# One unit of four and the mix of each row block transposed in float32 on TensorE instead of by DMA

## The chip, the cores and the metric

One core of a Trainium2 chip runs the whole program. The metric is the device time of one execution in microseconds. DMA stands for the core's sixteen DMA engines, SP for the engine that issues most of their transfers.

## The reference

One decoder layer is computed for a prompt of 1024 positions and for 8 single decode positions. The change lies in the prompt's attention and in what follows it:

```python
s_w = jnp.einsum('bqkgd,bskd->bqkgs', qi, wk[:, :, 0]) - sl5 * dist_w.astype(f32)[None, :, None, None, :]
o_w = jnp.einsum('bqkgs,bskd->bqkgd', masked_softmax(s_w, mask_w[None, :, None, None, :]), wk[:, :, 1])
...
o = gf[..., 0:1] * o_c + gf[..., 1:2] * o_s + gf[..., 2:3] * o_w
...
mix = jnp.concatenate([ya * jax.nn.silu(za), yb * jax.nn.silu(zb), yc * jax.nn.silu(zc)], axis=-1)
out = jnp.einsum('bte,ed->btd', mix, w_out)
return x + rms_norm(out, g_post).astype(x.dtype)
```

There are 8 heads of 64 and three branches: compressed (`o_c`), selected (`o_s`, here every block up to the position) and a window of 512 (`o_w`). All inputs and outputs are float32.

## The kernel before

Every float32 matmul is made of float16 ones: an operand is split into a high half (the float16 rounding) and a low half (the rest), and three products of halves are added. So each probability matrix and each mixed row exists twice in float16, high and low.

Attention starts at about 251 us. The 1024 positions are 8 row blocks of 128, taken in the order 7, 6, 2, 1, 0, 5, 4, 3 (`ROWS`, L1286). A row block is cut into **units** `u = (i, s0, nh)` of `nh` heads from head `s0`: one head each in rows 7 to 3, two in rows 2 and 1, four in row 0, 50 units in all (L1620). A unit of row i has `nh * nt` blocks of 128 x 128 probabilities, where `nt` is i + 1 plus min(i + 1, 5): 13, 12, 11, 10 and 8 for rows 7 to 3, 6 x 2, 4 x 2 and 2 x 4 for rows 2, 1, 0. The loop at L1660 runs a pipeline of four steps:

- `qk` (L1295): TensorE forms scores in PSUM tiles `s` of the pool `sp`, which has two slots of 128 x 1024. VectorE subtracts distances and takes the row bound (L1344), which frees the tile; ScalarE takes exponentials (L1346) into `P` and then copies all of `P`, scaled, to the float16 tile `H` (L1348).
- `high` (L1351): SP issues a DMA transpose of `H` into the first half of the tile `T` (L1355).
- `low` (L1358), one step later: VectorE forms `L`, the low half (L1362), and SP issues its DMA transpose into the second half of `T` (L1363).
- `pv` (L1382), three steps after `qk`: for each block three TensorE matmuls `O<-vn,T`, two with the high half and one with the low, into a tile of the pool `op`.

After four heads, `combine` (L1407) scales the sums (L1415); after eight, `finish` (L1418) adds the branches (L1422, L1423), multiplies by the gate `z` (L1425), and splits the product into halves (ScalarE L1429, VectorE L1431) that a DMA transpose (L1432) turns into `qa[:, i]`, the left operand of the output projection.

`outproj` (L1516) does 48 matmuls `op` of 128 x 512 for a row, 24 with pooling and gating rows (`mxg`, `mxp`) and 24 with `qa`. Projections of weights (`ps`), the pooling and gating branches and `outproj` are filler, which the loop hands out between units. The output weights are loaded by POOL's queue and split by ScalarE and VectorE (L1469).

The orders of TensorE, VectorE and ScalarE are set by a list scheduler in the framework, which goes by an estimate of times; SP and POOL keep the order of the program text. On every engine instructions run in order, so one that waits holds up those behind it. `fp` and `op` are two PSUM pools of two one-bank tiles each.

Of the kernel before, what the change touches and what calls it, by code (L numbers as in the profile page):

```python
# [10 lines left out]
F32 = mybir.dt.float32  # L11
F16 = mybir.dt.float16
I32 = mybir.dt.int32
AF = mybir.ActivationFunctionType
ALU = mybir.AluOpType
# [12 lines left out]
CE = {}  # L28
# [22 lines left out]
def tile_hymba(ctx: ExitStack, tc: tile.TileContext, A: dict):  # L51
    nc = tc.nc
    V, S, G, Y = nc.vector, nc.scalar, nc.gpsimd, nc.sync
    PS = bass.MemoryType.PSUM

    fp = ctx.enter_context(tc.tile_pool(name="fp", bufs=2, space=PS))
    sp = ctx.enter_context(tc.tile_pool(name="sp", bufs=2, space=PS))
# [8 lines left out]
    def mm(out, l, r, st, en):  # L66
        nc.tensor.matmul(out, lhsT=l, rhs=r, start=st, stop=en)  # L67
# [90 lines left out]
    qa = C.tile([128, 8, 8, 128], F16, name="qa")  # L158
# [38 lines left out]
    mp = D.tile([128, 2, 16], F32, name="mp")  # L197
# [208 lines left out]
    for c in range(3):  # L406
        a, b = c * CH, c * CH + CH
# [859 lines left out]
    AT = tc.alloc_tile_pool(name="AT", bufs=1, side="right", reuse_waits="tile")  # L1267
# [13 lines left out]
    def load_qx(i, hf):  # L1281
        t = qx[i, hf] = AT.tile([128, 2, 128], F16, tag="qx", name=f"qx{i}{hf}", bufs=2)
        for k in range(2):
            Y.dma_start(t[64 - k * 64:128 - k * 64], qa[k * 64:k * 64 + 64, i, hf * 4 + k:hf * 4 + 4:2])
# [4 lines left out]
    def spans(i):  # L1289
        n = min(i + 1, 5)  # L1290
        return (0, i + 1, 0), (1, n, i + 1)

    sums = {}

    def qk(u):  # L1295
        i, s0, nh = u
        nt = i + 1 + min(i + 1, 5)
        P = AT.tile([128, nh, nt * 128], F32, tag="P", name=f"P{i}_{s0}", bufs=2)
        if s0 == 0:
            sums[i] = AT.tile([128, 8, 4], F32, tag="sm", name=f"sm{i}", bufs=2)  # L1300
        sm = sums[i]
        if s0 == 0:
            load_qx(i, 1)
        elif s0 == 4 and i != ROWS[-1]:
            load_qx(ROWS[ROWS.index(i) + 1], 0)
        for h in range(nh):
            s = s0 + h
            k = s % 2
            r = slice(k * 64, k * 64 + 64)
            rx = slice(64 - k * 64, 128 - k * 64)  # L1310
            qy = qx[i, s0 // 4][rx, s % 4 // 2]
            lone = i == 7 and s < PARAM["lone"]
            slope = 2.0 ** -(SLOTS[s][0] * 4 + SLOTS[s][1] + 1)
            ps = None
            banks = []
            cuts = []
            for br, n, o in spans(i):
                T = n * 128
                if ps is None or n > 4 or i > 3:
                    ps = sp.tile([128, 1024], F32, tag="s", name=f"s{i}_{s}_{br}")  # L1320
                    z = 0
                else:
                    z = 512
                lo = (i + 1 - n) * 128
                if i > 3:
                    w = T // 2 if br else max(T // 2, 384)
                    z = 512 - w
                    parts = ((z, lo, w), (512, lo + w, T - w))
                else:
                    parts = ((z, lo, T),)  # L1330
                for a, c0, w in parts:
                    mm(ps[:, a:a + w], qa[:, i, s], ka[br][:, k, c0:c0 + w], True, False)
                    cuts.append((ps, br, a, c0, w))
                banks.append((ps, z))
            for pz, br, a, c0, w in cuts:
                if a == 512 and not lone:
                    mm(pz[:, a:a + w], qy, klx[br][rx, c0 - (384, 0)[br]:c0 - (384, 0)[br] + w], False, True)
                else:
                    mm(pz[:, a:a + w], qa[r, i, s], kl[br][r, c0:c0 + w], False, True)
            for (br, n, o), (ps, z) in zip(spans(i), banks):  # L1340
                T = n * 128
                end = 1024 if br == 0 else 1664
                p = P[:, h, o * 128:o * 128 + T]
                V.tensor_tensor_reduce(p, ps[:, z:z + T], ctt[:, end - T:end], -slope, 3e38, ALU.add, ALU.min,  # L1344
                                       sm[:, s, br:br + 1])
                S.activation(p, p, AF.Exp, bias=sm[:, s, br:br + 1], scale=-1.0, accum_out=sm[:, s, 2 + br:3 + br])  # L1346
        H = AT.tile([128, nh, nt * 128], F16, tag="H", name=f"H{i}_{s0}", bufs=2)
        S.activation(H, P, AF.Copy, scale=1024.0)  # L1348
        return P, H

    def high(u, P, H):  # L1351
        i, s0, nh = u
        nt = i + 1 + min(i + 1, 5)
        pt = AT.tile([128, 2 * nh * nt, 128], F16, tag="T", name=f"T{i}_{s0}", bufs=3)
        Y.dma_start_transpose(out=pt[:, 0:nh * nt], in_=H.rearrange("p h c -> p (h c)"))  # L1355
        return P, H, pt

    def low(u, P, H, pt):  # L1358
        i, s0, nh = u
        nt = i + 1 + min(i + 1, 5)  # L1360
        L = AT.tile([128, nh, nt * 128], F16, tag="L", name=f"L{i}_{s0}", bufs=2)
        V.scalar_tensor_tensor(L, P, 1024.0, H, ALU.mult, ALU.subtract)  # L1362
        Y.dma_start_transpose(out=pt[:, nh * nt:2 * nh * nt], in_=L.rearrange("p h c -> p (h c)"))  # L1363
        return pt
# [42 lines left out]
    def combine(i, h):  # L1407
        ob = obank.pop((i, h)).rearrange("p (s r d) -> p s r d", r=2, d=64)
        sc = AT.tile([128, 4, 2], F32, tag="asc", name=f"as{i}_{h}", bufs=2)
        V.scalar_tensor_tensor(sc, sums[i][:, h * 4:h * 4 + 4, 2:4], 1e-30, invg[:, i, h * 4:h * 4 + 4, 1:3],  # L1410
                               ALU.max, ALU.mult)
        V.reciprocal(sc, sc)
        if h == 0:
            mts[i] = AT.tile([128, 8, 2, 64], F32, tag="mt", name=f"mt{i}", bufs=1)
        V.tensor_tensor(mts[i][:, h * 4:h * 4 + 4], ob, sc.unsqueeze(3).to_broadcast([128, 4, 2, 64]), ALU.mult)  # L1415
        return finish(i) if h else None

    def finish(i):  # L1418
        t2 = mts.pop(i)
        t = t2[:, :, 0]  # L1420
        h3 = lambda x: x.rearrange("p (s d) -> p s d", d=64)
        V.tensor_tensor(t, t, t2[:, :, 1], ALU.add)  # L1422
        V.tensor_tensor(t, t, h3(ocs.pop(i)), ALU.add)  # L1423
        z = yza_t["z"][:, i]
        V.tensor_tensor(t, t, h3(z), ALU.mult)  # L1425
        t4 = t.rearrange("p (h s) d -> p h s d", h=2)
        hl = z.bitcast(F16)
        h5 = hl.rearrange("p (h a s d) -> p h a s d", h=2, a=2, d=64)
        S.activation(h5[:, :, 0], t4, AF.Copy)  # L1429
        yield  # L1430
        V.tensor_tensor(h5[:, :, 1], t4, h5[:, :, 0], ALU.subtract)  # L1431
        Y.dma_start_transpose(out=qa[:, i], in_=hl)  # L1432
        hold[f"ma{i}"] = qa[:, i]

    wo = {}
# [185 lines left out]
    for i in ROWS:  # L1621
        nh = (4, 2, 2, 1, 1, 1, 1, 1)[i]
# [37 lines left out]
    for st in range(n + 3):  # L1660
        t0 = now[0]
        flush()
        u = units[st - 1] if 1 <= st <= n else None
        if st < n:
            pend[units[st]] = qk(units[st])
        if u is not None:
            pend[u] = low(u, *pend[u])
        if st < n:
            pend[units[st]] = high(units[st], *pend[units[st]])
        bg_step()  # L1670
        if st >= n:
            bg_step()
            take(5.2)
        else:
            i, s0, nh = units[st]
            size = nh * (i + 1 + min(i + 1, 5))
            now[0] += 0.19 * size
            owed = take(owed + (PARAM["s2"] * size if "O" in outp else PARAM["s1"]) - 0.19 * size)
            now[0] = max(now[0], t0 + 0.33 * size + 0.8)
        if st >= 3:  # L1680
            v = units[st - 3]
            pv(v, pend.pop(v))
            e = v[1] + v[2]
            if e % 4 == 0:
                run_post(lambda: combine(v[0], v[1] // 4))
            if e == 8:
                fill.append(outproj(v[0]))
# [171 lines left out]
```

## Time and profile before

| | before |
|---|---|
| median of 3 runs | 587.06 us (586.46 to 589.16) |
| profiled execution, its time | 585.29 us |
| its span, first to last instruction | 583.5 us |
| TensorE matmuls busy | 519.7 us (89%) |
| VectorE, ScalarE, POOL busy | 441.8, 323.8, 197.0 us |
| mean granted TensorE clock | 0.953 |
| DMA transposes of `H` and `L` | 50 and 50, median 3.9 and 4.2 us to landing |

Times in rows of the trace count from the span's start. A busy TensorE is not TensorE at its peak: matmuls are pipelined, and a record is longer than the spacing of two. "DMA share" is the mean busy share of the sixteen DMA engines.

### The profile page before, as it was taken

How to read it: one execution, taken by the hardware profiler on the slowest of the kernel's cores; microseconds unless marked ns; L12 is line 12 of the kernel's file. 1: busy time of each engine (PE TensorE's matmuls, PEld its weight loads, DVE VectorE, ACT ScalarE, POOL GpSimd, SP SyncE). 2: the span in 40 equal slices, each digit the busy share in tenths (PEclk: the TensorE clock that was granted, in tenths of full speed). 3: DMA queues.
4: the chain of work that ended last, by engine and by line, in shares of the span. 5: the costliest groups of instructions: out<-in, count | busy, mean ns of one | idle time of the engine just before them, and what ended most of it. 6: DMA issues, size and time to landing. Idle time of an engine off the chain costs nothing. (4 is left out here: it accounts for less than half of the span.)

```text
span 583.5 us, 14199 instructions
## 1 busy us (share of the span) xinstructions
PE 519.7 (89%) x5716; PEld 342.7 (59%) x5716; DVE 441.8 (76%) x747; ACT 323.8 (55%) x574; POOL 197.0 (34%) x157
## 2 busy tenths in 40 slices
PE   5889988899999999899999979674599999998974
PEld 3566655589768999666666545442355455454531
DVE  5986489996686667478986987896799788768741
ACT  6444145564553434439656756496487765756600
POOL 1893179403267000045929775132011010000000
PEclk9989999899999999999999998967589999999997
DMA  8613984855675112847898597999969999998952
GB/s 300 260 37 99 253 222 135 244 165 143 206 260 159 39 40 34 239 92 145 171 184 166 97 184 114 125 229 224 124 100 166 182 213 206 177 215 153 199 154 80
DMA packets 199428, 95.31 MB, mean 163 GB/s; under 512 B 168890, under 2 KB 187738, under 8 KB 199362
## 3 DMA queue, kind: packets, MB, share of 16 engines
q1 hardware_dynamic: 195474, 80.85, 65.2%
q0 software_dynamic: 3744, 13.29, 7.3%
q8 instruction: 44, 0.72, 0.5%
q10 hardware_dynamic: 144, 0.26, 0.1%
q14 instruction: 22, 0.18, 0.1%
HBM read 45.43 MB, written 11.86 MB: 98 GB/s over the span
## 5 line engine op out<-in xcount | busy, mean ns | idle before, releaser
L67 PE MATMUL ps<-xh,ws 128*128 128x344 f16 x768 | 175.7, 313 | 5.8 <-DVE t L492 4.3
L67 PEld LDWEIGHTS <-ws 128*128 128x128 f16 x1376 | 129.3, 100 | 87.3 <-issue 17.4
L1346 ACT ACTIVATE P<-P,sm 128x640 f32<-128x640 f32 (+7 forms) x128 | 92.8, 725 | 77.6 <-DVE sm L1344 77.2
L67 PE MATMUL ps<-xl,ws 128*128 128x344 f16 x384 | 120.0, 313 | 0.0
L1362 DVE SCALAR_TENSOR_TENSOR L<-P,H 128x1024 f16<-128x1024 f32 (+4 forms) x50 | 85.0, 1700 | 25.7 <-ACT H L1348 15.3
L1344 DVE CUSTOM_DVE_ANT_0 P<-s,ctt 128x640 f32<-128x640 f32 (+7 forms) x128 | 84.8, 699 | 13.2 <-PE s L67 12.7
L67 PE MATMUL O<-vn,T 128*128 128x64 f16 x1584 | 64.0, 198 | 26.3 <-DMA T<-L 17.1
L67 PEld LDWEIGHTS <-T 128*128 128x128 f16 x1584 | 57.6, 101 | 40.4 <-DMA T<-L 18.9
L67 PEld LDWEIGHTS <-qa 128*128 128x128 f16 (+1 forms) x612 | 44.7, 98 | 61.5 <-issue 33.5
L1348 ACT ACTIVATE H<-P 128x1024 f16<-128x1024 f32 (+4 forms) x50 | 66.3, 1325 | 1.1
L67 PEld LDWEIGHTS <-xh 128*128 128x128 f16 x768 | 60.3, 98 | 0.7
L67 PE MATMUL op<-wo,qa 128*128 128x512 f16 x192 | 46.4, 389 | 3.3 <-DMA qa<-yza 3.3
L67 PE MATMUL s<-ka,qa 128*128 128x384 f16 (+4 forms) x192 | 45.1, 324 | 3.9 <-DVE sm L1344 3.7
L67 PE MATMUL zps<-ws,xh 128*128 128x128 f16 x512 | 45.0, 219 | 0.0
L1534 POOL TENSOR_SCALAR sq<-sq 128x1 f32<-128x1 f32 x8 | 3.9, 492 | 119.4 <-ACT o L1565 119.4
L67 PE MATMUL zps<-ws,xl 128*128 128x128 f16 x256 | 43.6, 219 | 0.0
L67 PEld LDWEIGHTS <-xl 128*128 128x128 f16 x384 | 37.5, 98 | 1.1 <-issue 0.5
L255 ACT ACTIVATE ws<-raw 128x1024 f16<-128x1024 f32 x21 | 22.2, 1056 | 17.6 <-PE ps L67 12.2
L67 PE MATMUL s<-kl,qa 64*128 64x384 f16 (+5 forms) x100 | 30.2, 329 | 0.0
L67 PE MATMUL s<-klx,qx 64*128 64x384 f16 (+4 forms) x92 | 26.9, 323 | 0.0
L1073 POOL TENSOR_TENSOR t<-t,yzc 128x1032 f32<-128x1032 f32 x2 | 4.8, 2382 | 60.4 <-DVE t L492 60.4
L67 PE MATMUL op<-wo,mxg 128*128 128x512 f16 x96 | 24.8, 395 | 0.1
(333 smaller groups left out, 917.5 us busy)
## 6 DMA issues: line engine op xcount, KB each, us to landing
raw<-in_wt_dram SPq DMA_DIRECT2D x21, 512.0 KB, 4.5
wor<-in_wo_dram POOLq DMA_DIRECT2D x8, 512.0 KB, 7.3
xr<-in_xn_dram SPq DMA_DIRECT2D x8, 512.0 KB, 4.8
o_y_dram<-o SPq DMA_DIRECT2D x7, 512.0 KB, 3.9
cr<-in_ccmp_dram SPq DMA_DIRECT2D x24, 128.0 KB, 3.3
o_kww_dram<-in_cwin_dram POOLq DMA_DIRECT2D x8, 259.0 KB, 4.5
o_kww_dram<-in_cwin_dram POOLq DMA_DIRECT2D x8, 252.0 KB, 4.8
xq<-in_xT_dram SPq DMA_DIRECT2D x3, 516.0 KB, 7.6
```

Of the source, the lines that this page charges most:

```text
L67: nc.tensor.matmul(out, lhsT=l, rhs=r, start=st, stop=en)
L255: S.activation(ws[:, 0, :, a:b], r, AF.Copy, scale=64.0)
L1073: G.tensor_tensor(t, t, hold.pop(f"zc{f2}"), ALU.mult)
L1344: V.tensor_tensor_reduce(p, ps[:, z:z + T], ctt[:, end - T:end], -slope, 3e38, ALU.add, ALU.min, sm[:, s, br:br + 1])
L1346: S.activation(p, p, AF.Exp, bias=sm[:, s, br:br + 1], scale=-1.0, accum_out=sm[:, s, 2 + br:3 + br])
L1348: S.activation(H, P, AF.Copy, scale=1024.0)
L1362: V.scalar_tensor_tensor(L, P, 1024.0, H, ALU.mult, ALU.subtract)
L1534: G.tensor_scalar(sq[:, 2:3], sq[:, 1:2], 1.0 / 1024, sq[:, 0:1], ALU.mult, ALU.add)
```

## The change

For one unit of four (the last head of each group of four in rows 7 to 3, the last unit in rows 2, 1 and 0: 13 units), `H`, `L` and both DMA transposes go. TensorE transposes `P` itself, in float32, block by block against an identity matrix, into tiles `tp` of the pool `sp`, up to eight blocks in one. ScalarE copies from there to the high half of `T`, and VectorE forms the low half. In `finish` of every row the gated product stays in float32 in `z`; TensorE transposes it in four blocks into a tile of `fp` (named `mp`), and ScalarE and VectorE split it out of PSUM into `qa`. The identity is loaded by SP before the first unit.

```diff
+    ident = AT.tile([128, 128], F32, name="ident")
+    Y.dma_start(ident, A["ce"][:, CE["ident"][0]:CE["ident"][0] + 128])
+
+    def by_pe(u):
+        i, s0, nh = u
+        return (s0 + nh) % 4 == 0 if i > 2 else s0 + nh == 8
...
+        if by_pe(u):
+            return P, None
         H = AT.tile([128, nh, nt * 128], F16, tag="H", name=f"H{i}_{s0}", bufs=2)
         S.activation(H, P, AF.Copy, scale=1024.0)
...
+        if by_pe(u):
+            return P, None, pt
         Y.dma_start_transpose(out=pt[:, 0:nh * nt], in_=H.rearrange("p h c -> p (h c)"))
...
+        if by_pe(u):
+            Pf = P.rearrange("p h c -> p (h c)")
+            for g in range(0, nh * nt, 8):
+                m = min(8, nh * nt - g)
+                tp = sp.tile([128, 1024], F32, tag="s", name=f"tp{i}_{s0}_{g}")
+                for j in range(m):
+                    nc.tensor.transpose(tp[:, j * 128:j * 128 + 128], Pf[:, (g + j) * 128:(g + j) * 128 + 128], ident)
+                t3 = tp.rearrange("p (j q) -> p j q", q=128)[:, 0:m]
+                hi = pt[:, g:g + m]
+                S.activation(hi, t3, AF.Copy, scale=1024.0)
+                V.scalar_tensor_tensor(pt[:, nh * nt + g:nh * nt + g + m], t3, 1024.0, hi, ALU.mult, ALU.subtract)
+            return pt
...
-        V.tensor_tensor(t, t, h3(z), ALU.mult)
-        t4 = t.rearrange("p (h s) d -> p h s d", h=2)
-        hl = z.bitcast(F16)
-        h5 = hl.rearrange("p (h a s d) -> p h a s d", h=2, a=2, d=64)
-        S.activation(h5[:, :, 0], t4, AF.Copy)
+        V.tensor_tensor(h3(z), t, h3(z), ALU.mult)
         yield
-        V.tensor_tensor(h5[:, :, 1], t4, h5[:, :, 0], ALU.subtract)
-        Y.dma_start_transpose(out=qa[:, i], in_=hl)
+        tp = fp.tile([128, 512], F32, tag="f", name=f"mp{i}")
+        for j in range(4):
+            nc.tensor.transpose(tp[:, j * 128:j * 128 + 128], z[:, j * 128:j * 128 + 128], ident)
+        t4 = tp.rearrange("p (a b q) -> p a b q", a=2, b=2)
+        m = qa[:, i].rearrange("p (a h b) q -> p a h b q", a=2, h=2)
+        S.activation(m[:, :, 0], t4, AF.Copy)
+        yield
+        V.tensor_tensor(m[:, :, 1], t4, m[:, :, 0], ALU.subtract)
```

The new text also moves instructions. On SP, from the last unit of row 2 to the third of row 1 (`T2_6` is the tile of row 2, head 6), there stood before:

```order
L1355 DMA_TRANSPOSE T2_6_5759<-H2_6_5754 128x12x128
L1284 DMA qx11_5849<-qa_87 64x2x128 x2
L1363 DMA_TRANSPOSE T2_6_5759<-L2_6_5872 128x12x128
L1355 DMA_TRANSPOSE T1_0_5875<-H1_0_5870 128x8x128
L1432 DMA_TRANSPOSE qa_87<-yza_2544 128x8x128
L1363 DMA_TRANSPOSE T1_0_5875<-L1_0_5959 128x8x128
L1355 DMA_TRANSPOSE T1_2_5962<-H1_2_5957 128x8x128
L1284 DMA qx00_6019<-qa_87 64x2x128 x2
L1363 DMA_TRANSPOSE T1_2_5962<-L1_2_6042 128x8x128
```

and in the same place stands now:

```order
L1284 DMA qx11_5901<-qa_87 64x2x128 x2
L1365 DMA_TRANSPOSE T1_0_5942<-H1_0_5922 128x8x128
L1385 DMA_TRANSPOSE T1_0_5942<-L1_0_6030 128x8x128
L1365 DMA_TRANSPOSE T1_2_6033<-H1_2_6028 128x8x128
L1284 DMA qx00_6091<-qa_87 64x2x128 x2
L1385 DMA_TRANSPOSE T1_2_6033<-L1_2_6114 128x8x128
```

Both transposes of row 2's last unit are gone, and so is the mix's, which stood between the two halves of row 1's first unit.

On VectorE, at the end of the program (what a row waits for stands in brackets), there stood before:

```order
L1362 SCALAR_TENSOR_TENSOR L3_7_8204<-P3_7_8144,H3_7_8154 128x1024 [waits DMAHW1_49,Activation_49]
L1566 TENSOR_TENSOR o324_8234<-op40_8166,gpb_6229 128x512 [waits Activation_49]
L1568 TENSOR_SCALAR sq4_8165<-sq4_8165 128x1
L1566 TENSOR_TENSOR o324_8234<-op41_8221,gpb_6229 128x512 [waits Activation_49]
L1415 TENSOR_TENSOR mt3_8140<-O3_1_8179,as3_1_8328 128x512 [waits DVE_49,PE_49]
L1539 SCALAR_TENSOR_TENSOR o324_8234<-o324_8234,sq4_8165,xr4_8163 128x1024 [waits DMAHW5_49,DVE_49,Pool_49]
L1422 TENSOR_TENSOR mt3_8140<-mt3_8140 128x8x64 [waits DVE_49]
L1423 TENSOR_TENSOR mt3_8140<-mt3_8140,ocs3_7942 128x8x64 [waits DVE_49]
L1425 TENSOR_TENSOR mt3_8140<-mt3_8140,yza_2544 128x8x64 [waits DVE_49]
L1431 TENSOR_TENSOR yza_2544<-mt3_8140,yza_2544 128x2x256 [waits Activation_49]
```

and now:

```order
L1590 TENSOR_TENSOR o324_8388<-op40_8312,gpb_6305 128x512 [waits DMAHW0_49,Activation_49]
L1592 TENSOR_SCALAR sq4_8311<-sq4_8311 128x1
L1381 SCALAR_TENSOR_TENSOR T3_7_8306<-tp3_7_0_8350,T3_7_8306 128x1024 [waits DMAHW7_49,DMAHW2_49,Activation_49]
L1590 TENSOR_TENSOR o324_8388<-op41_8375,gpb_6305 128x512 [waits Activation_49]
L1437 TENSOR_TENSOR mt3_8289<-O3_1_8325,as3_1_8482 128x512 [waits DVE_49,PE_49]
L1563 SCALAR_TENSOR_TENSOR o324_8388<-o324_8388,sq4_8311,xr4_8309 128x1024 [waits DMAHW6_49,DVE_49,Pool_49]
L1444 TENSOR_TENSOR mt3_8289<-mt3_8289 128x8x64 [waits DVE_49]
L1445 TENSOR_TENSOR mt3_8289<-mt3_8289,ocs3_8078 128x8x64 [waits DVE_49]
L1447 TENSOR_TENSOR yza_2544<-mt3_8289,yza_2544 128x512 [waits DVE_49]
L1456 TENSOR_TENSOR qa_87<-mp3_8489,qa_87 128x2x256 [waits Activation_49]
```

The low half of the last unit comes out of the PSUM tile `tp`, after one more step of row 4's output; the multiplication writes `yza` itself, and the last subtraction reads the PSUM tile `mp`. On TensorE the last unit's O matmuls are now followed by 12 projections of row 3, the four transposes into `mp`, 12 more projections, and the 24 that read `qa`. Row 7's mix is transposed within row 6, row 6's, 2's and 1's by the first units of row 5.

## Rows read from the trace of the kernel before

**Rows 1.** The page, busy tenths in 40 slices of the span.

```profile
PE   5889988899999999899999979674599999998974
PEclk9989999899999999999999998967589999999997
DMA  8613984855675112847898597999969999998952
```

**Rows 2.** Windows: length; PE, PEld, DVE, ACT, POOL busy; PEclk; DMA share; GB/s.

```profile
251.00:345.00 94.00, 90.64 (x1043) 59.22 (x1042) 80.70 (x116) 60.50 (x88) 66.20 (x31) 1.00 0.77 146
345.00:374.00 29.00, 25.36 (x301) 16.07 (x299) 22.99 (x53) 20.09 (x43) 9.77 (x10) 0.94 0.90 140
374.00:437.00 63.00, 39.66 (x435) 23.23 (x433) 50.08 (x130) 43.95 (x106) 13.04 (x13) 0.70 0.93 164
437.00:555.00 118.00, 114.42 (x1186) 59.97 (x1185) 93.96 (x175) 77.89 (x148) 8.37 (x13) 1.00 1.01 187
555.00:583.50 28.50, 16.65 (x121) 7.72 (x117) 8.79 (x15) 2.69 (x7) 1.61 (x4) 0.88 0.44 120
```

**Rows 3.** Timeline of TensorE at the decode step's four transposes; that window's row.

```profile
168.90 0.65 PE L817 MATMUL s<-cet,stl 128*128 128x128 f32 x4
...
169.39 0.31 PE L67 MATMUL ps<-xh,ws 128*128 128x344 f16 x1
...
168.00:170.50 2.50, 2.50 (x37) 2.01 (x35) 2.30 (x10) 0.55 (x3) 2.34 (x1) 1.00 1.01 390
```

**Rows 4.** Groups by line and shape: copies and splits, from SBUF and from PSUM.

```profile
L1348 ACT ACTIVATE H<-P 128x1664 f16<-128x1664 f32 x8 | 12.7, 1583 | 0.1
L1348 ACT ACTIVATE H<-P 128x1024 f16<-128x1024 f32 x14 | 14.8, 1054 | 0.3
L1362 DVE SCALAR_TENSOR_TENSOR L<-P,H 128x1024 f16<-128x1024 f32 x14 | 16.9, 1210 | 8.1 <-DMA T<-L 6.1 <-ACT H L1348 2.0
L576 ACT ACTIVATE thd<-cpsd 128x1024 f32<-128x1024 f32 x8 | 8.1, 1017 | 10.1 <-DVE ms L579 10.1
L577 DVE SCALAR_TENSOR_TENSOR thd<-thd,cpsd 128x1024 f32<-128x1024 f32 x8 | 9.7, 1215 | 0.0
```

**Rows 5.** Groups by line in 251 to 345: TensorE's first score matmuls.

```profile
L67 PE MATMUL s<-ka,qa 128*128 128x320 f16 (+2 forms) x59 | 13.7, 331 | 3.4 <-DVE sm L1344 3.3
```

**Rows 6.** Groups by line in 374 to 437; ScalarE's wait, from the list of waits.

```profile
L67 PE MATMUL O<-vn,T 128*128 128x64 f16 x228 | 13.2, 224 | 18.6 <-DMA T<-L 10.7 <-DMA T<-H 7.8
L67 PE MATMUL pp<-mxp,wpl 128*128 128x344 f16 x15 | 4.6, 436 | 4.4 <-ACT ocs L1380 4.4
...
ACT dsh L1162 <- DMA o_ps_dram<-dsh: 4.7, 1, 4.7
```

**Rows 7.** Timeline of SP's queue, 397 to 404: start, time in issue.

```profile
397.66 6.46 SPq L1432 DMA_TRANSPOSE qa<-yza  x1
```

**Rows 8.** The chain that ended last, in order of time: start, us, what.

```profile
552.71 0.04 ACT H L1348
...
565.72 0.64 ACT yza L1429
...
566.38 0.70 DVE yza L1431
...
567.10 3.04 DMA qa<-yza
570.18 6.96 PE op L67 x24
```

**Rows 9.** Timeline of TensorE at the end; in brackets the idle time before.

```profile
555.20 2.75 PE L67 MATMUL op<-wo,qa 128*128 128x512 f16 x12
557.79 0.92 PE L67 MATMUL O<-vn,T 128*128 128x64 f16 x26
560.89 0.81 PE L67 MATMUL O<-vn,T 128*128 128x64 f16 x22 [2.18 <-DMA T<-L]
...
570.18 6.94 PE L67 MATMUL op<-wo,qa 128*128 128x512 f16 x24 [3.29 <-DMA qa<-yza]
```

## The prediction

> **What bounds the kernel now.** I began with the forty slices [rows 1]: TensorE is at nine tenths in most of the second half, with a hole from slice 24 to 29 where its granted clock falls as well, while the DMA row stays near nine. Then I cut the attention, which is all that the change touches, into stages by the windows view [rows 2]; the reader is to see four different limits. In 251 to 345 (rows 7 and 6 with the last projections) TensorE is busy 90.6 of 94 us at full clock. In 374 to 437 (the end of row 2, rows 1 and 0, loading of the output weights) it is busy 39.7 of 63 us at a mean clock of 0.70; VectorE has 50 us, ScalarE 44, and the DMA share is 0.93. In 437 to 555 (rows 5, 4, 3 with the output projections) it is busy 114.4 of 118 us at full clock, and the DMA share is 1.01. After 555 comes a tail. The groups by line inside the hole say what TensorE waits for there: 18.6 us before the O matmuls, all of it for DMA transposes, and 4.4 us before a pooling matmul [rows 6]. The chain of waits and TensorE's timeline give the tail [rows 8, 9].
>
> **The change, part by part.** 13 of 50 units lose their two DMA transposes: two in each of rows 7, 6, 5, 4, 3 and one in each of rows 2, 1, 0. Their blocks number 2 x (13+12+11+10+8) + 12 + 8 + 8 = 136, so 136 float32 transposes are added on TensorE, and 8 x 4 = 32 for the mix. In all 26 + 8 DMA transposes with 272 + 64 blocks go, and one 64 KB load is added, issued before the first unit and first used after the fourth, which I cost at nothing.
>
> *One transpose.* The decode step already has four of this form. The first starts at 168.90 and the next matmul at 169.39 [rows 3]: 0.12 us each, at full clock. A bound below is the 0.11 us from the last record's start to that matmul; above, twice 0.12 at the half clock. I take 0.12, the same form at the clock that both full stages have. The Trainium skill (TensorE: Matmul & The Clock Gate, Part 4: PE-mode transpose) gives about 275 ns for a transpose in a kernel. The trace differs, since four share half a microsecond; with 0.275 as the spacing the sum below would be some 15 us higher.
>
> *Rows 7 and 6.* 50 transposes, and the four of row 7's mix: 54 x 0.12 = 6.5 us on an engine that is full. TensorE does wait 3.4 us there for VectorE to free a score tile [rows 5], all of it in row 6, so the 24 transposes of row 6 (2.9 us) hide in that: +3.6 us. Ends: 0, if the DMA's relief gives as much back, and +6.5.
>
> *The end of row 2, rows 1 and 0.* 28 transposes and about 12 of mixes, 4.8 us (9.6 at half clock), lie in 23 us of idle TensorE: nothing. What is gained is waiting. The most that transposes can cost the DMA is found in 251 to 345, if its whole 0.77 x 94 = 72 us [rows 2] is put on the 360 blocks transposed there: 0.20 us a block. Three units and two or three mixes leave the hole, some 56 + 24 blocks, up to 16 us of its 0.93 x 63 = 59 us of DMA. The mix's transpose also holds the SP queue 6.46 us, and the low half of row 1's first unit is issued only after it [rows 7]. Bounds: no gain, if other units' transposes land no sooner, and 23 us, both waits of rows 6. (The second hangs on a ScalarE copy behind another that waited 4.7 us for a store of the pooling state on the same queue.) With a quarter of the DMA work gone and the queue free I take half, -11.5 us.
>
> *Rows 5, 4, 3.* 58 + 12 = 70 transposes, 8.4 us. TensorE idles 3.6 of 118 us, so nothing hides them: +8.4 us. Ends: +2, if the DMA at 1.01 is what really paces this stage, and +16.8 at half clock.
>
> *ScalarE and VectorE.* The high copy and the low subtraction stay, but in 22 pieces for 13 units and out of PSUM. Out of PSUM 1024 columns take 1.02 and 1.22 us, out of SBUF 1.05 and 1.21 [rows 4]: the same. Nine more pieces on each cost the fixed part, from 1664 against 1024 columns on ScalarE 0.2 us: 1.9 us on engines that are busy 66 and 80% in 437 to 555. Nothing, while TensorE is the cover; if it were not, 1.9 us. The mix keeps its multiply, copy and subtraction in another order.
>
> *The tail.* Before, TensorE works without a gap to 558.7, waits 2.18 us for the last unit's low half, works to 566.9, waits 3.29 us for the mix, and needs 6.96 us for its last 24 matmuls [rows 8, 9]. Twelve such matmuls take 2.59 us at full clock (555.20 to 557.79), so 24 take 5.2; 1.8 us are the clock, which is granted in full again only during them. Removable: 2.2 + 3.3 + 1.8 = 7.3 us. With the change the last exponential ends at 552.7; eight transposes, a copy and a split (1.0 + 1.05 + 1.22) end by 556.5, before TensorE is free. From the last O matmul to the end of VectorE's chain are 4.0 us (561.7 to 565.7), and only 12 matmuls, 2.6 us, stand ahead of the mix's transposes: 1.4 us of waiting, and 0.5 for the four. ScalarE's copy and VectorE's subtraction (0.64 + 0.70) lie under the next twelve. So -7.3 + 1.9 = -5.4 us, between 0 and -7.3.
>
> *Sum.* The profiled execution took 585.29 us (span 583.5): +3.6 - 11.5 + 8.4 - 5.4 = -4.9, 580.4 us. The runs' median is 587.06, 1.8 above it; the same difference gives **582.2 us**, 0.8% faster. Of itself it lies within 577 to 588.
>
> **The rivals.** *A score tile is held too long (slower).* The transposes take tiles of the pool `sp`, whose two slots serve the scores. A score tile is freed after one VectorE pass; a transposed one after a copy and a split, 1.05 + 1.22 = 2.3 us, some 1.5 us longer [rows 4]. The next unit's first scores queue behind that on TensorE, and VectorE, ScalarE and the next units behind them. For it: 3.4 us of this wait exist already [rows 5]. Against it: in rows 5 to 3 TensorE's order has output projections between. It makes the kernel slower by over 0.5% once a quarter of 22 x 1.5 = 33 us is uncovered; at a third the time is 593 us.
>
> *The hole is paced by VectorE and ScalarE (no change).* They are busy 50 and 44 of 63 us and split the output weights there; a quarter of the waits goes, not a half. Then -5.7 in place of -11.5: 588 us.
>
> *DMA paces more than the hole (faster).* Its share is 1.01 in 437 to 555. If half of the 8.4 us there is given back and the hole gains 16 us in place of 11.5, it is 573.5 us.
>
> *The transposes do not keep the clock up (slower).* The four in rows 3 ran inside a stretch granted in full, too few to tell. If each ran at the half level, those that I count as visible (30 + 70) would cost 0.12 us more: 594 us. The same part of that Trainium skill page says that the full clock doesn't engage for transposes. The trace agrees in nothing so far, since four short ones left it at 1.00.
>
> That the change doesn't do what it says is excluded by the order: the DMA transposes are gone from SP, the new ones stand on TensorE.
>
> **How the numbers follow.** Forecast 0.52, long-held score tiles 0.13, the hole paced by VectorE and ScalarE 0.17, DMA pacing more 0.14, the clock 0.04. A measurement of this kernel tells about 0.5%, 2.9 us, from no change. Of the forecast's own 0.52, 0.33 is faster by more (its middle is 2 us beyond that bound), 0.16 within, 0.03 slower; the VectorE case splits 0.11 within and 0.06 slower; DMA pacing is all faster, the other two slower. Sum: 0.47, 0.27, 0.26. The range leaves out the clock, half of the score tiles' case and the outer part of the fast case: 573 to 593 us.
>
> **What would show it.** Right: O's wait for T in the hole down from 18.6 to about 9 us; the stage of rows 5, 4, 3 some 8 us longer with TensorE still full at clock 1.00; new transposes about 0.12 us apart; the chain's end without DMA transposes, and the last 24 projections in about 5.2 us. Wrong: TensorE waiting more than 3.4 us for VectorE before scores; a granted clock under 1.00 in rows 7, 6 or 5 to 3; a hole as long as now. The prediction falls most easily on the hole, where I chose half of a wait.

## The result, and the profile after

The kernel became slower: 595.38 us median (592.85 to 595.98, 4 runs) against 588.11 us (586.46 to 589.17, 4 runs) for the kernel before, a ratio of 1.015 (95% interval 1.011 to 1.020). That is +1.5% where -0.8% was forecast. In all ratios here, executions over 1.5% above the fastest of the same kernel are left out, and of dep_only, whose profile fell on one of these, only times are used. The profiled execution of the changed kernel took 595.98 us, its span 594.2 us.

The page of the changed kernel: TensorE's busy time, and the forty slices that answer to [rows 1].

```profile
PE 539.9 (91%) x5884; PEld 364.8 (61%) x5884; DVE 442.1 (74%) x756; ACT 323.8 (54%) x583; POOL 191.3 (32%) x157
...
PE   5989988998999999899999989847789999997995
...
PEclk9999998998999999999999999877798999998898
DMA  8613984854675113847577466768347857376552
```

TensorE's busy time rose by 20.2 us and the DMA row fell from near nine to near six in the second half, as a change of the transposes' engine should show. The hole is shallower: slices 24 to 29 read 796745 before and 898477 now. New in the second half are the eights of the clock row in slices 31, 37 and 38, where nines stood.

Up to the first scores the two programs are alike, yet these come at 251.7 us in the one profile and at 254.8 in the other. Over the kernels below that point moves between 251.7 and 257.8 us. In hole_split, which up to there does what the kernel before does, it lies at 255.1, so it isn't put down to the change, and I cut the stages by what is computed: from VectorE's first pass over the scores of row 7, of row 2, of row 5, to TensorE's end. Windows (columns as in [rows 2]), first of the kernel before:

```profile
251.73:357.11 105.38, 98.86 (x1144) 64.46 (x1143) 87.68 (x131) 68.57 (x100) 71.18 (x39) 0.98 0.79 148
357.11:433.07 75.96, 52.14 (x525) 30.76 (x524) 62.06 (x159) 52.15 (x128) 17.17 (x16) 0.75 0.94 157
433.07:577.12 144.05, 134.99 (x1403) 70.68 (x1402) 104.48 (x192) 83.22 (x159) 9.17 (x15) 0.99 0.92 177
```

and of the changed kernel:

```profile
254.75:357.81 103.06, 100.47 (x1164) 66.28 (x1163) 83.23 (x131) 67.43 (x101) 67.38 (x38) 1.00 0.63 121
357.81:432.90 75.09, 56.31 (x584) 37.83 (x581) 60.04 (x159) 51.82 (x130) 16.48 (x16) 0.82 0.62 130
432.90:587.70 154.80, 147.19 (x1503) 82.42 (x1498) 110.13 (x204) 84.72 (x165) 7.82 (x15) 0.97 0.60 129
```

Rows 7, 6 are 2.3 us shorter and rows 2, 1, 0 are 0.9 us shorter, -3.2 us in place of the forecast -7.9 (filler moves between the two: 72 weight projections stand in rows 2, 1, 0 now, 53 before; so their sum is the sound number). Rows 5, 4, 3 with the tail are 10.8 us longer, in place of +3.0. Together that is +7.6 us, and the medians differ by 7.3; the two profiles differ by 3.0 us more, which lie ahead of the first scores. The last stage holds the loss, and it was the one in which everything seemed to be counted.

What TensorE waited for in 251 to 594 of the changed kernel (total, times, longest):

```profile
PE O L67 <- DMA T<-L: 10.4, 6, 3.3
PE O L67 <- DMA T<-H: 6.8, 2, 5.0
PE s L67 <- DVE T L1381: 4.3, 2, 3.1
PE s L67 <- DVE sm L1350: 3.4, 6, 0.9
PE mp L1451 <- DVE yza L1447: 1.4, 1, 1.4
```

The third row is new: scores that wait for VectorE to split a transposed tile. It is small, and only 1.1 us of it lie in rows 5 to 3. But a wait shows only where TensorE has nothing ahead of the waiting instruction. TensorE's timeline over one such place, between two units of row 4 (start, time, what):

```profile
500.13 0.44 PE L67 MATMUL s<-ka,qa 128*128 128x320 f16 x2
...
501.13 1.46 PE L67 MATMUL op<-wo,mxg 128*128 128x512 f16 x6
502.43 1.46 PE L67 MATMUL op<-wo,mxp 128*128 128x512 f16 x6
503.72 2.75 PE L67 MATMUL op<-wo,qa 128*128 128x512 f16 x12
...
507.02 1.25 PE L1377 MATMUL tp<-ident,P 128*128 128x128 f32 x10
508.11 0.98 PE L67 MATMUL O<-vn,T 128*128 128x64 f16 x28
...
510.87 2.75 PE L67 MATMUL op<-wo,qa 128*128 128x512 f16 x12
...
513.52 0.60 PE L67 MATMUL op<-wo,mxg 128*128 128x512 f16 x2
513.95 0.71 PE L67 MATMUL s<-ka,qa 128*128 128x384 f16 x4
```

and ScalarE's and VectorE's in the same stretch (idle time before in brackets):

```profile
508.09 1.30 ACT L1380 ACTIVATE T<-tp 128x1024 f16<-128x1024 f32 x2 [0.83 <-PE tp L1377]
513.66 0.60 ACT L1589 ACTIVATE o<-op 128x512 f32<-128x512 f32 x1 [4.27 <-PE op L67]
```

```profile
502.63 0.82 DVE L1350 CUSTOM_DVE_ANT_0 P<-s,ctt 128x640 f32<-128x640 f32 x1
...
509.15 1.56 DVE L1381 SCALAR_TENSOR_TENSOR T<-tp,T 128x1024 f16<-128x1024 f32 x2 [1.10 <-ACT T L1380]
514.38 0.69 DVE L1590 TENSOR_TENSOR o<-op,gpb 128x512 f32<-128x512 f32 x1 [3.68 <-ACT o L1589]
```

The next scores stand 13.8 us behind the last ones. The old scores are used up when VectorE's pass ends at 503.5. From 507.0, when the transposes start, both slots are held until VectorE's split ends at 510.7, and the scores come behind fourteen more projections after that. So the hold itself is 3.7 us; 3.6 us ahead of it and 3.2 us behind it are projections that the scheduler's order put there. Fifty output projections fill TensorE in all: it looks busy, while ScalarE and VectorE, which live on scores, idle 4.3 and 3.7 us. The projections used here can't be cover later. I measured in each profile the longest stretches from one score pass of VectorE to the next in rows 5 to 3: 7.2 us before; 12.4, 8.9 and 8.0 us after, each round a group of transposes.

Where TensorE then does idle, the clock follows. Windows of the changed kernel:

```profile
436.00:442.00 6.00, 4.07 (x70) 2.69 (x71) 6.00 (x11) 5.27 (x8) 0.00 (x0) 1.00 0.34 63
442.00:448.00 6.00, 5.37 (x127) 4.14 (x124) 6.00 (x11) 4.52 (x8) 0.00 (x0) 0.94 1.01 139
448.00:454.00 6.00, 5.86 (x88) 4.48 (x86) 5.77 (x15) 3.80 (x10) 0.11 (x1) 0.78 0.89 174
```

After 2.6 us of idle in twelve, the granted clock is down to a mean of 0.78, a mixture of its two levels, 1.2 and 2.4 GHz. A second fall in this stage, to 0.68 in 544 to 550, stands behind 3.0 us of waits for DMA transposes and not for a slot. Over the whole stage the mean is 0.97 against 0.99 before.

### The profile page after: what moved, and what is told of

Same layout as the page of the kernel before. It is cut to its first block, busy times and chain, and to the rows that moved or that the text cites. A ratio compares the mean times of both kernels' runs of the same rounds, so it can differ in the third digit from the quotient of the medians.

```text
span 594.2 us, 14525 instructions
## 1 busy us (share of the span) xinstructions
PE 539.9 (91%) x5884; PEld 364.8 (61%) x5884; DVE 442.1 (74%) x756; ACT 323.8 (54%) x583; POOL 191.3 (32%) x157
## 4 chain that ended last, share of the span: by engine, by line
PE 47%; DVE 19%; DMA 10%; issue 9%; SPq 7%; ACT 6%; POOL 1%; DVEq 0%; POOLq 0%; ACTq 0%
PE ps L67 13%; PE op L67 12%; PE zps L67 5%; PE s L67 4%; PE O L67 4%; DMA T<-L 4%; DVE P L1350 3%; DVE L L1384 3%; SPq L296 3%; PE v1ps L67 2%; ACT P L1352 2%; PE tp L1377 2%; ACT H L1356 1%; DMA xq<-in_xT_dram 1%; SPq L318 1%
## 5 line engine op out<-in xcount | busy, mean ns | idle before, releaser
L67 PE MATMUL O<-vn,T 128*128 128x64 f16 x1584 | 68.1, 199 | 18.1 <-DMA T<-L 10.4
L67 PEld LDWEIGHTS <-T 128*128 128x128 f16 x1584 | 60.2, 102 | 34.3 <-DMA T<-L 12.0
L1384 DVE SCALAR_TENSOR_TENSOR L<-P,H 128x1024 f16<-128x1024 f32 (+4 forms) x37 | 65.2, 1761 | 16.5 <-ACT H L1356 16.4
L1356 ACT ACTIVATE H<-P 128x1024 f16<-128x1024 f32 (+4 forms) x37 | 49.2, 1329 | 0.7
L67 PE MATMUL op<-wo,qa 128*128 128x512 f16 x192 | 44.8, 379 | 0.0
L1558 POOL TENSOR_SCALAR sq<-sq 128x1 f32<-128x1 f32 x8 | 2.6, 323 | 126.2 <-ACT o L1589 107.4
L255 ACT ACTIVATE ws<-raw 128x1024 f16<-128x1024 f32 x21 | 22.2, 1059 | 22.4 <-PE ps L67 16.2
L67 PE MATMUL s<-klx,qx 64*128 64x384 f16 (+4 forms) x92 | 28.4, 321 | 1.2 <-DMA qx<-qa 1.2
L1381 DVE SCALAR_TENSOR_TENSOR T<-tp,T 128x1024 f16<-128x1024 f32 (+4 forms) x22 | 21.1, 971 | 6.8 <-ACT T L1380 6.8
L1590 DVE TENSOR_TENSOR o<-op,gpb 128x512 f32<-128x512 f32 x16 | 11.1, 691 | 19.8 <-ACT o L1589 19.8
```

The source lines that it names most:

```text
L255: S.activation(ws[:, 0, :, a:b], r, AF.Copy, scale=64.0)
L1381: V.scalar_tensor_tensor(pt[:, nh * nt + g:nh * nt + g + m], t3, 1024.0, hi, ALU.mult, ALU.subtract)
L1558: G.tensor_scalar(sq[:, 2:3], sq[:, 1:2], 1.0 / 1024, sq[:, 0:1], ALU.mult, ALU.add)
L1590: V.tensor_tensor(o32[:, c], ps, outp["gpb"][:, c], ALU.mult)
```

## The experiments

Two theories at first. **Price**: each transpose costs TensorE its spacing wherever TensorE is full, and the gain in the hole is small. **Score slot**: the tiles `tp` stand in the two slots of the scores and hold up the next ones. Ratios are to the kernel before on the same chip, with the 95% interval.

| run | ratio | interval |
|---|---|---|
| mixes alone (mix_only) | 0.995 | 0.992 to 0.999 |
| units alone (units_only) | 1.041 | 1.038 to 1.045 |
| last unit and last mix alone (tail_only) | 0.992 | 0.988 to 0.995 |
| rows 2, 1, 0 alone (hole_only) | 0.999 | 0.995 to 1.003 |
| 136 transposes as extra work (price_only) | 1.002 | 0.998 to 1.006 |
| 272 (price_twice) | 1.011 | 1.008 to 1.013 |
| units not transposed at all (no_te) | 0.995 | 0.992 to 0.999 |
| that, with 136 transposes as extra work (no_hold) | 0.995 | 0.992 to 0.999 |
| rows 2, 1, 0 not transposed (hole_free) | 0.984 | 0.980 to 0.988 |
| VectorE without the weights' low halves (hole_split) | 0.993 | 0.989 to 0.996 |
| five units of rows 5 to 3 back on DMA (no_mid) | 1.000 | 0.996 to 1.003 |
| `tp` in the pool `fp` (tp_fp) | 1.019 | 1.015 to 1.023 |
| `tp` free after ScalarE's copy (short_hold) | 1.022 | 1.017 to 1.027 |
| `tp` held, no wait for exponentials (hold_only) | 1.010 | 1.006 to 1.014 |
| wait for exponentials, nothing held (dep_only) | 1.006 | 1.002 to 1.010 |

**Which part of the change.** Four kernels with a smaller choice of units and mixes (`mix_pe` picks the mixes; the others keep the DMA transpose):

```diff
     def by_pe(u):
-        return (s0 + nh) % 4 == 0 if i > 2 else s0 + nh == 8
+        return False                                # mix_only; all mixes
+        return (s0 + nh) % 4 == 0 if i > 2 else s0 + nh == 8    # units_only; no mix
+        return i == 3 and s0 == 7                   # tail_only; mix i == 3
+        return i < 3 and s0 + nh == 8               # hole_only; mixes i < 3
```

> Only the mixes go by TensorE (32 transposes); all 50 units keep both DMA transposes. Theory of the price (each transpose costs TensorE its spacing of 0.12 us where TensorE is full, and what is left of the loss is clock and waits): at most 32 x 0.12 = 3.8 us, less the tail's 3.3 us of waiting for the mix and 1.7 us of clock, so 1 to 3 us faster than before, 585 to 587. Theory of the score slot (the tiles tp, which stand in the two slots of the scores, make the loss): no such tile is left, so the whole of the tail's gain shows, 4 to 6 us faster. If the mixes are what costs, slower than before.

> Only the 13 units go by TensorE (136 transposes); the mixes go by DMA as before. Both theories: nearly all of the loss is here. Price: 136 x 0.12 = 16.3 us, less what lies in the idle of rows 2, 1, 0 (28 transposes, 3.4 us), less 2.2 us of the last unit's wait and some 5 us gained in rows 2, 1, 0, so +5 to +8 us against before, 593 to 596. If instead the mixes make the loss, within 2 us of before.

> Only the last unit (row 3, head 7) and the last mix go by TensorE: 8 + 4 transposes. Price: 12 x 0.12 = 1.4 us against the removed waits of 2.2 and 3.3 us and 1.7 us of clock, with 1.4 us of a new wait before the mix: 3 to 5 us faster than before, 583 to 585. Rival (the tail's waits come back as others, since ScalarE and VectorE stand between): within 1 us of before.

> Only the last unit and the mix of each of rows 2, 1, 0 go by TensorE: 28 + 12 transposes. Price with the hole held up by DMA transposes: 3 to 6 us faster than before, 582 to 585. Rival (rows 2, 1, 0 are held up by VectorE and ScalarE, which split the output weights there; a transpose that lands earlier is followed by another wait): within 2 us of before. Score slot: slower by 1 to 3 us, from TensorE waiting for the split of a tile tp before the next scores.

Tail_only gained 0.85%, 5.0 us (3.0 to 6.9), and is the version that beats both kernels; until the last unit its order on TensorE is that of the kernel before. Its end on TensorE:

```profile
557.42 1.46 PE L67 MATMUL op<-wo,mxp 128*128 128x512 f16 x6
560.32 0.66 PE L1465 MATMUL mp<-ident,yza 128*128 128x128 f32 x4 [1.44 <-DVE yza L1461]
...
563.40 5.34 PE L67 MATMUL op<-wo,qa 128*128 128x512 f16 x24
```

Mix_only gained 0.5%, 2.8 us, which fits the price best and excludes neither. Hole_only gained nothing that can be measured, as its rival had it; why, and whether the score slot cost 1 us there, its interval doesn't tell. Units_only missed by far: +4.1% where +1% was expected. With the mixes on DMA, the scheduler made an order with a stretch of 16.2 us without a score pass; O waited 29.8 us for DMA transposes, though there were fewer of them, and the last mix 5.9 us:

```profile
PE O L67 <- DMA T<-H: 18.2, 10, 5.2
PE O L67 <- DMA T<-L: 11.6, 8, 3.1
PE op L67 <- DMA qa<-yza: 5.9, 1, 5.9
```

Why this order is so much worse than that of the full change wasn't separated. The mixes are worth 0.5% by themselves, yet the same 13 units cost 4.1% here and 1.5% in the full change. So the order that comes with a change can weigh as much as the change, and it stays a rival in all that follows.

**TensorE's price, and the rest without it.** In price_only and price_twice extra transposes run into the score tile that the scores overwrite; in no_te the units' `T` is filled from SBUF.

```diff
+        if extra(u) and h == br == 0:                # price_only, price_twice (2 * nh * nt)
+            for j in range(nh * nt):
+                nc.tensor.transpose(ps[:, 0:128], ident, ident)
```

```diff
-                tp = sp.tile([128, 1024], F32, tag="s", name=f"tp{i}_{s0}_{g}")
...
-                t3 = tp.rearrange("p (j q) -> p j q", q=128)[:, 0:m]
+                t3 = Pf.rearrange("p (j q) -> p j q", q=128)[:, g:g + m]        # no_te
```

> The kernel before, with its DMA transposes, plus the same number of transposes on TensorE at the same 13 units (136), all of the identity, into the score tile that the scores then overwrite: no score slot is held longer, nothing waits for them, no DMA is saved. Theory of the price: rows 7 and 6 have 50, rows 5 to 3 have 58, at 0.12 us, less the 3 us that TensorE idles there: 8 to 11 us slower than before, 594 to 598, which is the whole loss of the change. Theory of the score slot: an extra matmul costs little beside the holding; within 4 us of before. If a transpose costs its 0.27 us record, 25 us or more slower.

> The kernel before with two extra transposes of the identity per block at the 13 units (272 in place of 136), into the score tile before the scores. The run with 136 measured a ratio of 1.002 (0.998 to 1.006). If TensorE is what bounds rows 7 and 6 and rows 5 to 3 and the spacing of 0.115 us adds up: the second 136 cost 116 x 0.115 = 13 us, ratio 1.02 to 1.03. If those stages have slack that takes TensorE work (DMA or VectorE paces them as much): ratio 1.003 to 1.012.

> The changed kernel, in which the 13 units aren't transposed at all: ScalarE and VectorE fill both halves of T from P in SBUF, so neither TensorE's 136 transposes nor the tiles tp in the score slots are there (T holds untransposed blocks); the mixes stay on TensorE. Theory of the price: 10 to 14 us less than the changed kernel, 581 to 585. Score slot: the same, since both go; with the run of the price alone it tells which. If the order that the scheduler makes of the new program is what costs, it stays above 590.

The price theory falls as an account of the whole loss. 136 transposes added to the kernel before can't be measured, and 272 cost 6.2 us (4.9 to 7.6), some 0.02 us each. The windows of price_twice show where they went:

```profile
362.62:435.89 73.27, 57.36 (x622) 38.35 (x622) 63.22 (x164) 55.86 (x134) 14.84 (x16) 0.88 0.96 171
435.89:583.18 147.29, 142.96 (x1518) 82.67 (x1518) 106.12 (x193) 82.84 (x158) 8.33 (x15) 1.00 0.85 172
```

In the last stage 116 transposes at 0.11 us should add 12.8 us and add 3.2: idle time fell from 9.1 to 4.3 us, and the clock is 1.00 throughout. No_te came out 2.0% under the changed kernel, 12 us, as expected of both theories.

**The hole.** hole_free takes all ten units of rows 2, 1, 0 off any transposing; hole_split takes 9.7 us off VectorE there.

```diff
-            V.scalar_tensor_tensor(w[:, 1], raw, 64.0, w[:, 0], ALU.mult, ALU.subtract)
+            G.memset(w[:, 1], 0.0)                   # hole_split
```

> The kernel before, in which none of the ten units of rows 2, 1, 0 is transposed: no DMA transposes and no TensorE work for them (T holds untransposed blocks, filled by ScalarE and VectorE); the mixes by DMA. If DMA transposes hold up the hole, as the prediction had it: 10 to 20 us faster than before, 567 to 577. If VectorE, ScalarE and the loads of the output weights hold it up: within 4 us of before, with O's wait for T gone and other waits in its place.

> The kernel before, in which VectorE doesn't form the low halves of the output weights (GpSimd fills them with zeros): 8 passes of 1.2 us, 9.7 us of VectorE in the hole go; all DMA transposes stay. If VectorE paces the hole: 4 to 9 us faster than before, 578 to 583. If DMA transposes do: within 2 us of before.

With no transposes at all for ten units the kernel gains 1.6%, 9.6 us: the stage took 63.04 us, and O waits for VectorE (5.0 us) and ScalarE (3.6 us) in place of the DMA. That is just short of the 10 to 20 us of a hole held up by DMA transposes. So -11.5 us for three of ten units was about what all ten give (7.2 to 12.0 us in time, 12.9 us in the stage). Hole_split is inconclusive: its time fell by 0.75%, but its profile has the stage at 76.05 us, as before, and O waiting 20.2 us there, so what the time gained isn't shown to be VectorE's work in the hole.

**Slot or dependency.**

```diff
-        return (s0 + nh) % 4 == 0 if i > 2 else s0 + nh == 8
+        return s0 % 4 == 3 and (i > 5 or (i, s0) == (3, 7)) if i > 2 else s0 + nh == 8    # no_mid
...
-                tp = sp.tile([128, 1024], F32, tag="s", name=f"tp{i}_{s0}_{g}")
+                tp = fp.tile([128, 512], F32, tag="f", name=f"tp{i}_{s0}_{g}")    # tp_fp, m <= 4
```

> The changed kernel, with the nine units of rows 5, 4, 3 ahead of the last one... six of them less the last, that is five, back on DMA transposes (both units of rows 5 and 4, the first of row 3); rows 7, 6, 2, 1, 0, the last unit and all mixes stay on TensorE. If the loss is made in rows 5 to 3 (their transposes, the held score slots and the clock): 11 to 14 us less than the changed kernel, ratio to before 0.990 to 0.995. If the units of rows 7 and 6 share it by their number of blocks: 6 to 8 us less, ratio 1.000 to 1.005.

> The changed kernel, with the units' transposes in tiles of the pool fp (one bank, four blocks at a time) in place of the score pool: the same TensorE work, no score slot is taken, more and smaller copies and splits (38 pieces in place of 22). Score slot: the waits of scores for the split are gone, and with them the clock that they cost; 4 to 9 us less than the changed kernel, ratio to before 0.997 to 1.006. Price of TensorE alone: as the changed kernel, ratio 1.01 to 1.02. If the slots of fp, which the output projections use, are held instead: over 1.02.

Of no_mid's text, "five" is the number of units. Five units back on DMA bring 1.6%, 9 us, between the two expectations. The stages say where:

```profile
256.81:359.97 103.16, 100.45 (x1164) 66.27 (x1163) 83.23 (x131) 67.43 (x101) 67.38 (x38) 1.00 0.63 121
359.97:434.40 74.43, 55.11 (x585) 36.90 (x582) 60.35 (x159) 51.83 (x130) 16.48 (x16) 0.84 0.62 131
434.40:579.87 145.47, 139.88 (x1453) 76.38 (x1448) 108.90 (x200) 84.80 (x161) 8.79 (x15) 0.95 0.79 159
```

The first two are those of the changed kernel within 0.7 us, and the last is 9.3 us shorter: the loss sits in rows 5 to 3. Tp_fp at 1.019 was no better than the changed kernel, which seems to speak against the slot; but `fp` serves the output projections, and stretches of 13.2 and 11.4 us without a score pass stand in rows 5 to 3 of its profile, whose last stage takes 159.5 us. It seems to have moved the hold and not removed it. The next four are to separate the two:

```diff
+    nc.tensor.transpose(ps[:, 0:128], ident, ident)              # no_hold: no_te + price_only
+    nc.tensor.transpose(ps[:, 0:128], Pp[:, j * 128:j * 128 + 128], ident)   # dep_only; Pp: P of the unit before
-    nc.tensor.transpose(tp[:, j * 128:j * 128 + 128], Pf[:, (g + j) * 128:(g + j) * 128 + 128], ident)
+    nc.tensor.transpose(tp[:, j * 128:j * 128 + 128], ident, ident)          # hold_only
```

```diff
-    V.scalar_tensor_tensor(pt[:, nh * nt + g:nh * nt + g + m], t3, 1024.0, hi, ALU.mult, ALU.subtract)
+    V.scalar_tensor_tensor(pt[:, nh * nt + g:nh * nt + g + m],
+        Pf.rearrange("p (j q) -> p j q", q=128)[:, g:g + m], 1024.0, hi, ALU.mult, ALU.subtract)   # short_hold
```

> The run without the units' transposes (no_te), with 136 transposes of the identity put back into the score tile before the scores: TensorE, ScalarE and VectorE have as many instructions as in the changed kernel, the DMA transposes are gone as there, but no tile tp is held and no probability goes through PSUM (T holds untransposed blocks). If TensorE's work is the loss: ratio to before 1.010 to 1.020, as the changed kernel. If the held tile and the way from TensorE over ScalarE and VectorE back to the scores are: no_te's 0.995 and 1 to 4 us, 0.997 to 1.003.

> The changed kernel, in which VectorE forms the low half from P in SBUF and not from the tile tp (the low halves of the 13 units hold untransposed blocks): the same instructions on every engine, but tp is free after ScalarE's copy, some 1.05 us and not 2.3 us after the last transpose. If the held score slot makes the loss: 3 to 7 us less than the changed kernel, ratio 1.003 to 1.010, and the scoreless stretches at the transposes in rows 5 to 3 (8.9, 12.4, 8.0 us) shorter. If the way over ScalarE is enough to make it, or the order that the scheduler finds: 1.012 to 1.020.

> The changed kernel, in which the 136 transposes read the identity and not P (T of the 13 units holds no probabilities): the tiles tp are held in the score slots as in the changed kernel, with the same copies and splits out of PSUM, but TensorE waits for no exponential before them. If the held slot and the way tp, copy, split, next scores make the loss: ratio 1.010 to 1.022. If the wait of TensorE's transposes for the exponentials does: 0.994 to 1.003, as in the run without both (0.995).

> The run no_hold (0.995), in which the 136 transposes read P of the unit before in place of the identity: they stand in TensorE's order ahead of the scores of the next unit and wait for the exponentials of P, but no tile is held and nothing is read back from them (T holds untransposed blocks). If TensorE's wait for the exponentials makes the loss: ratio 1.008 to 1.022. If the held slot does: 0.994 to 1.003.

No_hold does the TensorE work of the change, has its relief of the DMA, and takes 0.995 of the time before: what the change loses, it loses on the way through PSUM and by the order that comes with it. Windows of no_hold, then rows 2, 1, 0 and the last stage of no_te, then the last stage of hold_only:

```profile
257.00:359.37 102.37, 98.40 (x1163) 67.12 (x1162) 88.31 (x130) 65.83 (x97) 70.23 (x38) 1.00 0.66 123
359.37:428.70 69.33, 51.12 (x583) 33.77 (x582) 63.05 (x159) 52.24 (x131) 16.76 (x17) 0.88 0.67 136
428.70:575.55 146.85, 143.57 (x1497) 80.63 (x1495) 108.68 (x203) 86.17 (x170) 10.45 (x15) 0.99 0.65 137
```

```profile
360.76:435.46 74.70, 50.35 (x519) 30.51 (x518) 63.01 (x157) 50.05 (x126) 12.79 (x15) 0.74 0.60 120
435.46:577.31 141.85, 138.02 (x1438) 74.86 (x1437) 107.29 (x201) 85.87 (x167) 8.08 (x15) 0.98 0.67 142
```

```profile
432.63:587.33 154.70, 146.12 (x1488) 81.56 (x1487) 108.40 (x199) 83.77 (x166) 8.17 (x15) 0.97 0.59 128
```

No_hold and no_te take the same time, but their last stages don't: with the same other work, the stage with 58 transposes more is 5.0 us longer, 0.09 us each. Rows 2, 1, 0 are 5.4 us shorter in no_hold and hide it. So with the DMA share at 0.65, where price_twice had 0.85, most of the price was paid in that stage; whether the DMA is the reason wasn't tested.

Holding tiles that wait for nothing gives the last stage of the changed kernel back to 0.1 us: 154.7, with the clock at 0.97 and score-free stretches of 12.5 and 11.3 us. Without the hold it is 146.9, with none over 7.4 us. The last stage keeps to this in the other profiles: it takes 154.7 to 165.6 us in the three kernels with all 13 units' tiles in the score slots for copy and split (the changed kernel, hold_only, units_only), and 139.2 to 147.3 us in those with none or few there (tail_only the shortest, price_twice the longest). In the time, the hold is worth 1.5% (0.995 to 1.010) and the wait for exponentials 1.0% (0.995 to 1.006); together they are a little more than the 2.0% to explain. Hold_only lies at the lower end of its expectation and dep_only between its two (it has 128 transposes, since no unit follows the last), so the two shares are rough. Short_hold missed its expectation: its time didn't fall, and its interval lies above the changed kernel's median: its last stage is down to 147.9 us, as the slot would have it, but rows 7 and 6 take 105.9 us, and in rows 2, 1, 0, now 79.4 us, O waits 10.2 us at one DMA transpose. Each of these kernels has an order of its own, so what the hold costs by itself and what the order round it costs stays open.

## Why the prediction was wrong

**Rows 5, 4, 3: the step that failed.** The sum had +8.4 - 5.4 = +3.0 us and nothing for the held score tiles; without the hold no_hold measures 146.85 - 144.05 = +2.8, with it the change measures +10.8. That +2.8 comes so near to +3.0 is luck, for no_hold has twelve projections in this stage that stood ahead of it before (first line before, second no_hold):

```profile
L67 PE MATMUL op<-wo,qa 128*128 128x512 f16 x180 | 43.6, 390 | 3.3 <-DMA qa<-yza 3.3
L67 PE MATMUL op<-wo,qa 128*128 128x512 f16 x192 | 45.8, 389 | 0.0
```

At the prediction's 2.59 us for twelve, no_hold is at +0.2 on like work: the tail's -4.9, and some 5 us for transposes in place of 8.4. The hold, with the order round it, thus costs 8 us, on like work more. This is the rival "a score tile is held too long", put at 0.13 and 593 us. I set it aside because "in rows 5 to 3 TensorE's order has output projections between". They are between, but they don't hide the hold: the scores stand behind them, ScalarE and VectorE run dry, and the cost comes back as idle time (7.6 us against 3.3) and in 3.6 us more of busy TensorE. The clock is lower too (0.97 against 0.99), but its share isn't shown: no_mid's last stage had 0.95 and took 145.5 us. The sign that I named, more than 3.4 us of TensorE waiting for VectorE before scores, came in all (4.3 + 3.4 us) but hardly in this stage. The rival's price was near, its working not: it counted exposed waits. The Trainium skill (Perfetto Trace Analysis, Matmuls) wants independent matmul groups rotated through PSUM banks, so that one's evacuation overlaps the next one's matmuls. Here two slots had to carry scores and transposes, and the trace agrees: hold_only's last stage is 7.9 us longer than no_hold's.

**The price per transpose.** The spacing was as read in [rows 3]: the ten at 507.02 take 1.25 us with a last record of some 0.28, 0.11 us each. Adding it up over every full stage was too much. A TensorE at 90.6 of 94 us busy [rows 2] still took extra transposes: price_only has 1.002 in time. The +8.4 us was thus an upper end, of which no_hold against no_te shows 5.0 us. For the +3.6 us no gain or loss is shown: rows 7 and 6 got 2.3 us shorter, with 19 weight projections fewer in them. I also counted 16 mix transposes after the start of row 5, the last four among them, where there are 20.

**The hole.** -11.5 us was the largest term and rested on half of a wait. The stage measures 75.1 us against 76.0, the long hole that I had named as a sign of being wrong. O's wait there fell from 18.6 us [rows 6] to 13.1 us and not 9, and the 4.4 us before the pooling matmul went, but 5.1 us before scores (0.4 before) and 1.2 us for `qx` came. In 374 to 437 of the kernel before, then of the changed one:

```profile
L67 PE MATMUL s<-ka,qa 128*128 128x256 f16 (+3 forms) x42 | 9.2, 312 | 0.4 <-DVE sm L1344 0.3
...
L67 PE MATMUL O<-vn,T 128*128 128x64 f16 x264 | 14.2, 218 | 13.1 <-DMA T<-L 7.3 <-DMA T<-H 5.0 <-ACT T L1380 0.8
L67 PE MATMUL s<-ka,qa 128*128 128x256 f16 (+3 forms) x42 | 8.8, 297 | 5.1 <-DVE T L1381 3.1 <-DVE sm L1350 1.9
```

Hole_only's 0.999 and hole_free's 9.6 us for all ten units bound it: three units' share would be 2.9 us, an estimate from the latter.

**The tail was right.** Forecast -5.4 us; tail_only measures -5.0 in time and 139.17 us against 144.05 in the stage. The new wait for the mix was put at 1.4 us and is 1.44, the last 24 projections at 5.2 us and are 5.34, in place of 6.96 [rows 8]. In the changed kernel the end is the same, with the wait 1.44 and the last 24 in 5.34 us; there the gain drowns.

**The clock** did drop below 1.00 in rows 5 to 3, but behind idle TensorE, not in transposes by themselves: with 116 of them price_twice has 1.00 in that stage. The rival of the slow transposes falls. The Trainium skill (TensorE: Matmul & The Clock Gate, A second HAM failure mode: psum-queue depth-cycling) tells of a kernel whose matmul groups cycle through PSUM banks with short idle times between them, and whose clock goes up and down between two levels. The fall here fits that in part: four waits of 0.15 to 1.13 us in 436 to 446, two for a transposed tile's copy or split and two for VectorE's score pass, then a mean of 0.78.

## What to carry to other kernels

Moving a transpose from DMA to TensorE trades a transfer that holds no PSUM slot against a PSUM tile that lives over three engines. In this kernel's last stage the tile, with the order round it, cost some 8 us and TensorE's time some 5. Ask first whose slot it takes and who stands behind that slot: filler on the waiting engine hides the wait in the profile, and the starved engines are where it shows. Where nothing follows, at the end of the program, the same exchange pays at once: tail_only is 0.85% faster than the kernel before.

## What was not expected of the hardware

Extra TensorE work in a half-idle stage went with a shorter stage and a higher clock. In rows 2, 1, 0 the mean granted clock was 0.75 before and 0.74 in no_te, 0.83 in price_only, and 0.88 in price_twice and no_hold; the stages took 76.0 and 74.7 us, 72.4 us, and 73.3 and 69.3 us. The extra work there was 28 or 56 transposes of 0.11 to 0.22 us, and in the last two there are more weight projections as well (72, against 53 before). Short_hold breaks the row: 0.83 and 79.4 us. These are single profiles, and orders differ between them; that the clock shortened the stage is an inference, not shown by itself.
